# The stick-breaking scores' high-part product: 128 rows with a zero-padded key in place of 64 rows

## The chip, the cores and the metric

The kernel runs on one core of one Trainium2 chip. The metric is the device time of one execution in microseconds, given as the median of several runs. A core has a matrix engine (TensorE, PE in the profile, with its weight loads shown apart as PEld), VectorE (DVE), ScalarE (ACT), GpSimd (POOL) and SyncE (SP), which here issues the weight DMAs. The engines run side by side and wait for each other through semaphores. Matrix products write to PSUM; all other tiles lie in SBUF.

## The reference, cut to what matters

The reference is one layer of a decoder trunk on 512 tokens of width 1024: a mixer of three branches (short convolution, stick-breaking attention, retention) merged under sigmoid gates, a cross-attention into 256 memory tokens, and a squared-ReLU MLP, with norms between. The change touches the scores `z` of the stick-breaking attention, which has 8 heads of 64 features:

```python
for start in range(0, s, SB_BLOCK):              # blocks of 128 queries
    end = start + SB_BLOCK
    z = jnp.einsum('bhtd,bhsd->bhts', q[:, :, start:end], k[:, :, :end]) * scale
    causal = s_idx < t_idx
    log_not = jnp.where(causal, jax.nn.log_sigmoid(-z), 0.0)
    between = lax.cumsum(log_not, axis=3, reverse=True) - log_not
    a = jnp.where(causal, jnp.exp(jax.nn.log_sigmoid(z) + between), 0.0)
    outs.append(jnp.einsum('bhts,bhsd->bhtd', a, v[:, :, :end]))
```

A block of queries sees the keys up to its own end, so the four blocks of a head have scores of 128, 256, 384 and 512 columns.

## The kernel before

**Arithmetic.** Products of float32 values are made from fp32r parts: each operand is kept as a high part (the value rounded to fp32r) and a low part (the rest), and a product is high x high + high x low + low x high. In the projections that is a helper, `mm3` (L232), whose three matmuls have the lines L234, L235 and L236; each has 128 partitions of contraction, 128 columns of weights and up to 512 columns of moving operand. Weight chunks of 512 KB arrive by DMA (L178) and are split into parts by ScalarE (L111) and VectorE (L112) ahead of their use.

**Scores.** A head has only 64 features, so the three terms of its score are made with two matmuls. `sq_done` (L455) writes, for each head of a pair, a tile with the query's high part on the head's own 64 partitions and its low part on the other 64. `sk_done` (L464) writes the key the other way round into `sb_k`: its low part on the head's own 64 partitions, its high part on the others. One matmul of `sb_q` against `sb_k` on all 128 partitions (L487) is therefore the sum of both cross terms. The high x high term comes first (L486), on the head's own 64 partitions alone, from `sb_q` and a third tile, `sb_kh`, with the key's high part. For head 0 of a pair these are partitions 0 to 63, for head 1 64 to 127. In both matmuls the query is the stationary operand (128 columns of weights), and both add into the same tile `z`.

**A step.** `sb_scores` (L479) makes `z` for a head and a block of queries; ScalarE and VectorE turn it into log weights, with a mask of the diagonal on GpSimd twice (`diag`, L474, on `sb_e` and on `sb_suf`) and a running sum between; `sb_transpose` (L505) transposes the weights `sb_suf` on TensorE (`aT`, L510) and splits them; `sb_out` (L525) multiplies them with `sb_v` (L544). There are 8 x 4 steps. They stand in the plan between the projections of the first part (the loop at L785), so that the steps' chains through the other engines run beside projections.

**Order.** The plan is written out by hand, but a scheduler then sets each engine's row by its own estimate of times; it may move instructions of different items past each other. Each engine works its row in order. Tiles come from pools with a fixed number of slots: 29 units of 4 KB for each partition for all that lives long (`unit`, L52), 10 scratch slots of 2 KB (`scr`, L55), and in PSUM four banks each for projections and attention. `sb_kh` is a scratch tile, `sb_q` and `sb_k` are units. A tile whose slot is still in use waits for its last reader.

**Later stages.** Products of 1024 x 256 x 512 under the gates and in the MLP's first half are made in seven smaller products (`seven`, L282, matmuls of 256 columns at L290), 18 double tiles in all (six of gates, twelve of hidden tiles); each takes four scratch tiles, and its consumer one or two more.

Of the kernel before, what the change touches and what calls it, by code (L numbers as in the profile page):

```python
# [15 lines left out]
P = 128  # L16
T = 512          # tokens
D = 1024         # model width
KT = D // P      # feature tiles of the model width
NT = T // P      # token tiles  # L20
MEM = 256
W = 512          # branch width
# [5 lines left out]
CW = 1024        # float32 per partition in one weight chunk (512 KB)  # L28

# columns of the packed small parameters  # L30
C_BG, C_CW, C_CB, C_RG = 0, 24, 36, 40
C_N = 44
UNITS, SCRS = 29, 10         # slots of 4 KB and of 2 KB per partition
RAWS, WBUFS, AHEAD = 3, 11, 2     # weight chunks loaded, parts of them, parts split ahead of their use
G7, U7 = 12, 8      # the first gate tile and the first hidden tile that go through seven products
# [3 lines left out]
def trunk_kernel(ctx: ExitStack, tc: tile.TileContext, x, mem, par, rot, dqd, kdec, g_mix, g_xa, g_mem, g_mlp,  # L39
# [11 lines left out]
    # one size for everything that lives longer than a few instructions: 4 KB per partition  # L51
# [12 lines left out]
    class Split:  # L64
        """[P, n * cols] float32 kept as its two fp32r parts, in units of 4 KB"""
# [49 lines left out]
    class Plain:  # L115
        """a chunk as it is"""
# [9 lines left out]
    class Seven:  # L126
        """two chunks [B11 | B12], [B22 | B21] as the seven right-hand blocks of a product"""
# [32 lines left out]
    class Stream:  # L160
        def __init__(self, entries):
            self.loads = [l for e in entries for l in e.loads]
            self.steps, first = [], 0       # (entry, step, first of its loads, loads needed)
            for e in entries:
                e.first = first
                for i, st in enumerate(e.steps):
                    self.steps.append((e, st, first + (len(e.loads) if i else 1)))
                first += len(e.loads)
                e.last = len(self.steps)
            self.raw = {}  # L170
            self.nd = self.ns = 0

        def load(self, n):
            """trace the loads of the first n chunks"""
            while self.nd < min(n, len(self.loads)):
                raw = wpool.tile([P, CW], F32, name="w_raw", bufs=RAWS)
                t, c = self.loads[self.nd]
                nc.sync.dma_start(out=raw, in_=t[c])  # L178
                self.raw[self.nd] = raw
                self.nd += 1  # L180

        def pump(self, n):
            """trace the loads and splits of the first n steps"""
            while self.ns < min(len(self.steps), n):
                e, fn, need = self.steps[self.ns]
                self.load(max(need, e.first + RAWS))
                e.parts.append(fn([self.raw[e.first + i] for i in range(len(e.loads)) if e.first + i in self.raw]))
                self.ns += 1

    plan = []       # (weight chunks, function that traces the work on them)  # L190
# [4 lines left out]
    def capture(build):  # L195
        """the items that build() adds, taken out of the plan"""
        n = len(plan)
        build()
        got = plan[n:]
        del plan[n:]  # L200
        return got
# [19 lines left out]
    def split(hi, lo, src):  # L221
        """hi + lo = src; src in SBUF or PSUM, float32."""
        act.copy(out=hi, in_=src)
        dve.tensor_tensor(out=lo, in0=src, in1=hi.bitcast(F32), op=ALU.subtract)

    def split_scaled(hi, lo, src, s):
        """hi + lo = src * s, s a power of two"""
        act.activation(out=hi, in_=src, func=AF.Copy, scale=s)
        dve.scalar_tensor_tensor(out=lo, in0=src, scalar=s, in1=hi.bitcast(F32),
                                 op0=ALU.mult, op1=ALU.subtract)  # L230

    def mm3(ps, lh, ll, rh, rl, first, last):  # L232
        """one K tile of a float32 product from its fp32r parts"""
# [7 lines left out]
    def proj_t(ps, w, a, sl=slice(None), nk=8, c0=0):  # L241
        """features on partitions: 128 columns of the chunk against the split activations a"""
# [5 lines left out]
    class Mixes:  # L248
        """the seven left-hand blocks of the split activations a, [P, 4 feature tiles, 256 tokens] each"""
# [6 lines left out]
        def make(self, g):  # L256
            """feature tiles 2 g, 2 g + 1 of the mixed blocks"""
# [24 lines left out]
    def seven(b, a):  # L282
        """two tiles of 128 features x 512 tokens, K = 1024, in seven products of half the size each way
        (Winograd's form); returns the first tile's halves and the second tile"""
# [27 lines left out]
    def proj_m(ps, ws, a, t, k0, nk):  # L312
        """128 tokens on partitions: 512 columns, chunks ws hold K tiles k0, k0 + 1, ..."""
# [8 lines left out]
    def items_m(src, c0, a, done, nt=NT, tok_outer=False):  # L322
        """512 output columns from four chunks; done(t, ps) takes each tile of 128 tokens"""
# [21 lines left out]
    def rstd_of(ms, n):  # L345
        """ms^-0.5 on [P, n]"""
# [4 lines left out]
    def sumsq(src, c, ss, dst):  # L351
        """ss[:, c] = sum of the squares of columns c * 512 ...; dst is scratch"""
# [9 lines left out]
    def norm_begin(key, src):  # L362
        """the left half's sum of squares"""
# [7 lines left out]
    def norm_end(key, src, g_bc):  # L371
        """xn = RMSNorm(src) * g for one tile of 128 tokens"""
# [5 lines left out]
    def norm_T(key, dst, t):  # L378
        """tile t of the normalised tokens, transposed and split"""
# [11 lines left out]
    S = {}          # what the phases hand on  # L391

    # ==== mixer: norm ====
# [25 lines left out]
    def item_t(fn, src, c, a=hT, sl=slice(None)):  # L419
        """one output tile with features on partitions; fn(ps) takes it"""  # L420
# [6 lines left out]
    sec = lambda i: 4 * i       # first chunk of section i of w_in  # L427

    # ==== stick-breaking attention ====
    # v of two heads... [token, tile, head, hi 64 | lo 64]  # L430
    def sv_alloc():
        S["v"] = [unit("sb_v", (P, 2, 4, 2 * SBD)) for _ in range(4)]    # [2 * group + tile pair]
# [17 lines left out]
    # Per head, on 128 partitions: the query's two parts, and the key's two parts the other way round  # L450
    # (their product is the two cross terms); the key's high part once more where the query's is.
    # The low half of a head pair keeps its high parts on partitions 0-63, the other on 64-127.
# [11 lines left out]
    def sk_done(m):  # L464
        def fn(ps):
            k = S["sk", m] = unit("sb_k")
            kh = S["skh", m] = scr("sb_kh", dt=F32R)
            act.copy(out=kh, in_=ps)
            for e, (own, oth) in enumerate(((LO, HI), (HI, LO))):
                act.copy(out=k[oth, e, :], in_=ps[own, :])  # L470
                dve.tensor_tensor(out=k[own, e, :], in0=ps[own, :], in1=kh[own, :].bitcast(F32), op=ALU.subtract)
        return fn

    def diag(ap):  # L474
        """keep s < t in a diagonal block"""
# [3 lines left out]
    def sb_scores(hd, tb):  # L479
        hp, e = divmod(hd, 2)  # L480
        q, k = S["sq", hp], S["sk", hp]
        rows = slice(64 * e, 64 * e + 64)
# [3 lines left out]
        te.matmul(z[:, :s], q[rows, e, tsl], S["skh", hp][rows, :s], start=True, stop=False)  # L486
# [5 lines left out]
        # softplus(z) = max(z, 0) + ln(1 + exp(-|z|))  # L492
# [3 lines left out]
        # suffix sums, the own column included: log of the weight is z - suf  # L496
# [28 lines left out]
    def sb_out(hd, tp):  # L525
        """output columns of token tiles 2 tp, 2 tp + 1 of one head"""
# [5 lines left out]
        ostart = [0, 1] if tp == 0 else [0, 3]       # where the two tiles' blocks start  # L532
# [30 lines left out]
    # ==== short convolution ====  # L563
# [27 lines left out]
    # ==== retention: projections ====  # L591
# [23 lines left out]
    # ==== order of the first part: attention steps between projections ====  # L615
# [28 lines left out]
    # ==== retention: recurrence ====  # L644
# [74 lines left out]
    # ==== branch projections under sigmoid gates ====  # L719
# [28 lines left out]
    def item_t7(fn, src, c, *chunks):  # L748
        """two output tiles in seven products; fn(e, halves, *ws) takes tile e as pairs (columns, source)"""
# [59 lines left out]
    # memory norm  # L809
# [10 lines left out]
    # tiles before G7 in full products, while the mixed blocks are made  # L820
# [9 lines left out]
    # ==== mixer output ====  # L830
# [9 lines left out]
    def proj_norm(src, a, g, after):  # L840
        """x += a @ src (1024 columns), and the norm that follows, tile by tile;
        after: what keeps TensorE at work until the last tile is there"""
# [18 lines left out]
    # ==== cross-attention ====  # L861
# [103 lines left out]
    # ==== squared-ReLU MLP ====  # L965
# [11 lines left out]
    def first_up(last_T):  # L977
        """the first tiles in halves of the tokens"""
# [41 lines left out]
    # ==== last projection and final norm, tile by tile ====  # L1020
# [24 lines left out]
def _tables():  # L1045
    """rotary and decay tables: they depend on the shapes alone"""
# [4 lines left out]
    cos, sin = np.cos(ang).T, np.sin(ang).T                      # [64, T]  # L1051
# [3 lines left out]
    rel = i[None, :] - i[:, None]                                # [j, i] -> i - j  # L1055
# [10 lines left out]
def _pack_t(w):  # L1066
    """[1024, N] -> chunks [N/128, 128, 8 * 128]"""
# [4 lines left out]
def _pack_s(w):  # L1072
    """[1024, N] -> chunks [N/128, 128, 2 * 512]: for 256 columns, halves of K and of the columns:
    [B11 | B12], [B22 | B21]"""
# [6 lines left out]
def _pack_m(w):  # L1081
    """[K, N] -> chunks [(N/512) * (K/256), 128, 2 * 512]"""
# [4 lines left out]
def _pack_b(w):  # L1087
    """[512, N] -> chunks [N/256, 128, 4 * 256]"""
# [60 lines left out]
```

## Time and profile before

| | |
|---|---|
| median of 3 runs | 1045.35 us (1045.32 to 1045.4) |
| span of the profiled execution (first to last instruction, which is all that the page gives of it) | 1043.7 us |
| median less span | 1.65 us |
| TensorE busy | 1027.0 us, 98% of the span |
| weight loads | 887.1 us, 85% |
| VectorE, ScalarE, GpSimd busy | 650.4 us (62%), 498.6 us (48%), 59.4 us (6%) |
| chain that ended last, by engine | PE 97%, DMA 1% |
| chain, lines L486 and L487 | 1% each |

The chain is followed back from the last instruction, at each step to what released it. Matmuls overlap in the pipeline: the durations of neighbours add up to more than the time they take together, so what one of them costs is read from the distance between starts, or from the chain, which counts each piece of time once. In the chain view a run of matmuls of one line is merged into one row with its count.

### The profile page before, as it was taken

What the parts mean: (1) busy time and instruction counts of PE and PEld (TensorE: products, weight loads), DVE (VectorE), ACT (ScalarE), POOL (GpSimd) and SP (SyncE); (2) the same over time, 40 slices, a digit from 0 to 9 for tenths busy, and PEclk for the clock granted to TensorE, in tenths of its full rate; (3) what the DMA queues carried; (4) which work ended last, traced back from release to release, by engine and by line L of the source; (5) the groups of instructions that cost most, each with busy time, mean ns of one, the idle gap of its engine ahead of it and who ended that gap; (6) DMA issues with size and microseconds to landing.
All of it is one profiled execution on the core that took longest, in us unless ns stands there. A gap on an engine that the chain in (4) does not pass through costs nothing.

```text
span 1043.7 us, 14329 instructions
## 1 busy us (share of the span) xinstructions
PE 1027.0 (98%) x5636; PEld 887.1 (85%) x5636; DVE 650.4 (62%) x992; ACT 498.6 (48%) x883; POOL 59.4 (6%) x110
## 2 busy tenths in 40 slices
PE   6999999999999999999999999999999999999997
PEld 4878888888888889998898888899889889989985
DVE  5567767765554597685585456365957566565643
ACT  5455556656633244454464445244425734643741
POOL 1001112221110000000010000000000000000000
PEclk9999999999999999999999999999999999999999
DMA  7321223212222213224645213222212322331322
GB/s 262 102 100 65 78 84 119 81 61 102 70 72 81 81 61 102 96 102 148 220 146 178 81 61 122 81 82 101 102 64 90 110 101 81 118 125 66 107 92 80
DMA packets 29875, 106.33 MB, mean 102 GB/s; under 512 B 3568, under 2 KB 3568, under 8 KB 29808
## 3 DMA queue, kind: packets, MB, share of 16 engines
q1 hardware_dynamic: 27216, 98.05, 26.6%
q10 hardware_dynamic: 2592, 7.37, 2.0%
q8 instruction: 44, 0.72, 0.3%
q14 instruction: 23, 0.19, 0.1%
HBM read 103.31 MB, written 2.10 MB: 101 GB/s over the span
## 4 chain that ended last, share of the span: by engine, by line
PE 97%; DMA 1%; DVE 0%; ACT 0%; SPq 0%; issue 0%; DVEq 0%; POOLq 0%; POOL 0%
PE mm L234 24%; PE mm L235 24%; PE mm L236 24%; PE p L290 17%; PE at L385 1%; PE z L486 1%; PE o L544 1%; PE z L487 1%; PE aT L510 1%; DMA w_raw<-in_w_in_dram 1%; PE xsc L236 0%; PE xsc L234 0%; PE xsc L235 0%; PE ro L691 0%; PE sc L665 0%; PE xpp L927 0%
## 5 line engine op out<-in xcount | busy, mean ns | idle before, releaser
L112 DVE TENSOR_TENSOR w_part<-w_raw,w_part 128x1024 fp32r<-128x1024 f32 (+1 forms) x180 | 210.7, 1175 | 171.3 <-PE mm L235 79.8
L111 ACT CAST w_part<-w_raw 128x1024 fp32r<-128x1024 f32 (+1 forms) x180 | 180.5, 1006 | 139.8 <-PE mm L236 83.9
L234 PE MATMUL mm<-hT_h,w_part 128*128 128x512 f32 (+1 forms) x512 | 193.7, 380 | 0.0
L235 PE MATMUL mm<-hT_l,w_part 128*128 128x512 f32 (+1 forms) x512 | 193.3, 378 | 0.0
L236 PE MATMUL mm<-hT_h,w_part 128*128 128x512 f32 (+1 forms) x512 | 192.9, 377 | 0.0
L290 PE MATMUL p<-mix_h,w_part 128*128 128x256 f32 x576 | 112.2, 283 | 0.5 <-ACT sv_s L297 0.5
L236 PEld LDWEIGHTS mm<-hT_h,w_part 128*128 128x128 f32 x512 | 96.4, 188 | 17.4
L235 PEld LDWEIGHTS mm<-hT_l,w_part 128*128 128x128 f32 x512 | 96.5, 188 | 16.5
L234 PEld LDWEIGHTS mm<-hT_h,w_part 128*128 128x128 f32 x512 | 96.2, 188 | 16.7
L235 PE MATMUL mm<-w_part,u_h 128*128 128x512 f32 x256 | 99.8, 390 | 0.0
L234 PE MATMUL mm<-w_part,u_h 128*128 128x512 f32 x256 | 98.8, 390 | 0.0
L236 PE MATMUL mm<-w_part,u_l 128*128 128x512 f32 x256 | 98.0, 389 | 0.0
L290 PEld LDWEIGHTS p<-mix_h,w_part 128*128 128x128 f32 x576 | 93.4, 192 | 1.4 <-ACT sv_s L297 0.7
L290 PE MATMUL p<-hT_h,w_part 128*128 128x256 f32 x432 | 84.4, 283 | 0.0
L290 PE MATMUL p<-mix_l,w_part 128*128 128x256 f32 x288 | 81.4, 283 | 0.0
L290 PEld LDWEIGHTS p<-hT_h,w_part 128*128 128x128 f32 x432 | 70.1, 192 | 0.8
L111 ACT CAST w_part<-w_mix 128x1024 fp32r<-128x1024 f32 x36 | 37.9, 1052 | 55.5 <-PE mm L235 37.4
L112 DVE TENSOR_TENSOR w_part<-w_mix,w_part 128x1024 fp32r<-128x1024 f32 x36 | 44.0, 1222 | 27.1 <-ACT w_part L111 20.0
L290 PE MATMUL p<-hT_l,w_part 128*128 128x256 f32 x216 | 60.7, 283 | 0.0
L236 PEld LDWEIGHTS mm<-w_part,u_l 128*128 128x128 f32 x256 | 48.1, 188 | 9.8
L235 PEld LDWEIGHTS mm<-w_part,u_h 128*128 128x128 f32 x256 | 48.1, 188 | 9.5
L234 PEld LDWEIGHTS mm<-w_part,u_h 128*128 128x128 f32 x256 | 47.9, 188 | 9.6
(210 smaller groups left out, 1808.5 us busy)
## 6 DMA issues: line engine op xcount, KB each, us to landing
w_raw<-in_w_in_dram SPq DMA_DIRECT2D x52, 512.0 KB, 3.4
w_raw<-in_w_up_dram SPq DMA_DIRECT2D x32, 512.0 KB, 3.5
w_raw<-in_w_down_dram SPq DMA_DIRECT2D x32, 512.0 KB, 3.5
w_raw<-in_w_br_dram SPq DMA_DIRECT2D x12, 512.0 KB, 3.4
w_raw<-in_w_gate_dram SPq DMA_DIRECT2D x12, 512.0 KB, 3.5
w_raw<-in_w_o_dram SPq DMA_DIRECT2D x8, 512.0 KB, 3.8
w_raw<-in_w_xk_dram SPq DMA_DIRECT2D x8, 512.0 KB, 4.5
w_raw<-in_w_xv_dram SPq DMA_DIRECT2D x8, 512.0 KB, 3.5
```

The lines of the kernel that those rows point to most:

```text
L111: act.copy(out=wh, in_=src)
L112: dve.tensor_tensor(out=wl, in0=src, in1=wh.bitcast(F32), op=ALU.subtract)
L234: te.matmul(ps, lh, rh, start=first, stop=False)
L235: te.matmul(ps, lh, rl, start=False, stop=False)
L236: te.matmul(ps, ll, rh, start=False, stop=last)
L290: te.matmul(ps[:, :256], x[:, k, :], y, start=first and k == 0 and i == 0, stop=k == 3 and i == 2, skip_group_check=True)
L385: te.transpose(ps[:, k * P:(k + 1) * P], xn[:, c * P:(c + 1) * P], ident)
L486: te.matmul(z[:, :s], q[rows, e, tsl], S["skh", hp][rows, :s], start=True, stop=False)
L487: te.matmul(z[:, :s], q[:, e, tsl], k[:, e, :s], start=False, stop=True)
L510: te.transpose(aps[:, sb * P:(sb + 1) * P], a[:, sb * P:(sb + 1) * P], ident)
L544: te.matmul(dst, vv, rhs, start=sb == 0 and i == 0, stop=sb == nblk and i == 1, skip_group_check=True)
```

## The change

`sb_kh` becomes a unit with a plane of 512 keys for each head of the pair. A plane holds the key's high part on the head's own 64 partitions and zeros on the other 64, where the query tile has its low part. The high x high matmul then takes all 128 partitions of both tiles. GpSimd writes the zeros, and ScalarE casts the high part in two pieces of 64 partitions instead of one of 128. The unit pool gets a slot more (30), the scratch pool one less (9). Otherwise the diff takes comments out and moves line numbers: L486 and L487 become L488 and L489, L476 becomes L479, and the aT matmuls of L510 are L512.

```diff
-UNITS, SCRS = 29, 10         # slots of 4 KB and of 2 KB per partition
...
+UNITS, SCRS = 30, 9
...
             k = S["sk", m] = unit("sb_k")
-            kh = S["skh", m] = scr("sb_kh", dt=F32R)
-            act.copy(out=kh, in_=ps)
+            kh = S["skh", m] = unit("sb_kh")
             for e, (own, oth) in enumerate(((LO, HI), (HI, LO))):
+                pool.memset(kh[oth, e, :].bitcast(F32), 0.0)
+                act.copy(out=kh[own, e, :], in_=ps[own, :])
                 act.copy(out=k[oth, e, :], in_=ps[own, :])
-                dve.tensor_tensor(out=k[own, e, :], in0=ps[own, :], in1=kh[own, :].bitcast(F32), op=ALU.subtract)
+                dve.tensor_tensor(out=k[own, e, :], in0=ps[own, :], in1=kh[own, e, :].bitcast(F32),
+                                  op=ALU.subtract)
...
-        rows = slice(64 * e, 64 * e + 64)
...
-        te.matmul(z[:, :s], q[rows, e, tsl], S["skh", hp][rows, :s], start=True, stop=False)
+        te.matmul(z[:, :s], q[:, e, tsl], S["skh", hp][:, e, :s], start=True, stop=False)
         te.matmul(z[:, :s], q[:, e, tsl], k[:, e, :s], start=False, stop=True)
```

On TensorE the row of the program is nearly the same. The clearest move is at the fourth step of head 0 (512 score columns; `aT` are the transposes of the third step). Before:

```order
L236 MATMUL mm<-hT_h,w_part 128x512
L510 MATMUL aT<-ident,sb_suf 128x128 x2
L486 MATMUL z<-sb_kh,sb_q 128x512
L487 MATMUL z<-sb_k,sb_q 128x512
L234 MATMUL mm<-hT_h,w_part 128x512
```

and now:

```order
L234 MATMUL mm<-hT_h,w_part 128x512
L512 MATMUL aT<-ident,sb_suf 128x128
L488 MATMUL z<-sb_kh,sb_q 128x512
L512 MATMUL aT<-ident,sb_suf 128x128
L489 MATMUL z<-sb_k,sb_q 128x512
L235 MATMUL mm<-hT_l,w_part 128x512
```

Between the score products of the third step and these stand 28 projection products where there were 24, and the two score products no longer stand next to each other: the second transpose is between them.

On ScalarE, at the key of the second head pair (`mm` is the projection's PSUM tile, `w_part` a weight chunk's high part, `sb_e` the softplus of the step at 256 columns). Before:

```order
L468 CAST sb_kh<-mm 128x512
L470 CAST sb_k<-mm 64x512
L111 CAST w_part<-w_raw 128x1024
L489 ACTIVATE sb_e<-z 128x256
L470 CAST sb_k<-mm 64x512
L490 ACTIVATE sb_e<-sb_e 128x256
```

and now:

```order
L471 CAST sb_kh<-mm 64x512
L472 CAST sb_k<-mm 64x512
L111 CAST w_part<-w_raw 128x1024
L491 ACTIVATE sb_e<-z 128x256
L471 CAST sb_kh<-mm 64x512
L472 CAST sb_k<-mm 64x512
L492 ACTIVATE sb_e<-sb_e 128x256
```

One cast more stands between the softplus' first and second function of the step.

On GpSimd the memsets of the first two head pairs, four of them, stand behind the first norm's work and ahead of all masks. The other two pairs stand among the masks. The third head pair's place before (numbers tell the tiles apart):

```order
L476 AFFINE_SELECT sb_suf_1008<-sb_suf_1008 128x128
L476 AFFINE_SELECT sb_e_1072<-sb_e_1072 128x128
L476 AFFINE_SELECT sb_suf_1078<-sb_suf_1078 128x128
L476 AFFINE_SELECT sb_e_1165<-sb_e_1165 128x128
L476 AFFINE_SELECT sb_suf_1171<-sb_suf_1171 128x128
```

and now:

```order
L479 AFFINE_SELECT sb_suf_1014<-sb_suf_1014 128x128
L479 AFFINE_SELECT sb_e_1078<-sb_e_1078 128x128
L470 MEMSET sb_kh_1157 64x512 x2
L479 AFFINE_SELECT sb_suf_1084<-sb_suf_1084 128x128
L479 AFFINE_SELECT sb_e_1174<-sb_e_1174 128x128
```

Two memsets stand between the two masks of one step.

## Rows read from the trace of the kernel before

**Rows 1.** Page, part 1: busy time, share of the span, instructions.
```profile
PE 1027.0 (98%) x5636; PEld 887.1 (85%) x5636; DVE 650.4 (62%) x992; ACT 498.6 (48%) x883; POOL 59.4 (6%) x110
```

**Rows 2.** TensorE's waits: total us, times, longest us.
```profile
PE at L385 <- DVE xn L376: 9.1, 2, 8.6
PE p L290 <- ACT sv_s L297: 0.5, 1, 0.5
```

**Rows 3.** Stretch with all score products: busy us of each engine (instructions), granted clock, DMA.
```profile
55.00:267.00 212.00, 212.00 (x979) 169.98 (x978) 144.90 (x215) 125.32 (x239) 35.96 (x73) 1.00 0.24 85
```

**Rows 4.** Timeline of TensorE, first score tile: start us, duration us, engine, line, tiles, rows*columns.
```profile
55.20 0.39 PE L234 MATMUL mm<-hT_h,w_part 128*128 128x512 f32 x1
55.52 0.32 PE L486 MATMUL z<-sb_kh,sb_q 64*128 64x128 f32 x1
55.77 0.50 PE L235 MATMUL mm<-hT_l,w_part 128*128 128x512 f32 x1
56.11 0.39 PE L236 MATMUL mm<-hT_h,w_part 128*128 128x512 f32 x1
...
56.80 0.39 PE L236 MATMUL mm<-hT_h,w_part 128*128 128x512 f32 x1
57.03 0.22 PE L487 MATMUL z<-sb_k,sb_q 128*128 128x128 f32 x1
...
57.37 0.39 PE L235 MATMUL mm<-hT_l,w_part 128*128 128x512 f32 x1
```

**Rows 5.** Timeline of the weight loads there; idle time before, in brackets.
```profile
54.98 0.19 PEld L234 LDWEIGHTS mm<-hT_h,w_part 128*128 128x128 f32 x1
55.52 0.18 PEld L486 LDWEIGHTS z<-sb_kh,sb_q 64*128 64x128 f32 x1 [0.35 <-issue]
```

**Rows 6.** Chain of work in four short stretches: start us, us, what.
```profile
62.10 0.31 PE z L486
...
62.95 0.23 PE mm L235
...
68.30 0.36 PE z L486
...
69.27 0.23 PE mm L235
...
74.71 0.42 PE z L486
...
75.80 0.23 PE mm L235
...
81.99 0.26 PE z L486
...
82.79 0.23 PE mm L236
```

**Rows 7.** Chain of 55 to 267 us by line; then 31 products of 256 columns.
```profile
by line: PE mm L235 27.4%; PE mm L236 27.3%; PE mm L234 27.3%; PE z L486 5.1%; PE z L487 4.8%; PE o L544 4.3%; PE aT L510 4.0%
...
423.98 3.72 PE p L290 x31
```

**Rows 8.** Casts and subtraction of the key: count, ns min/median/max, first and last start us.
```profile
L470 ACT CAST sb_k<-mm x8: 577/581/586, 51.3 to 190.6; 64x512 fp32r<-64x512 f32 x8
L471 DVE TENSOR_TENSOR sb_k<-mm,sb_kh x8: 672/688/695, 51.9 to 191.2; 64x512 fp32r<-64x512 f32 x8
...
L468 ACT CAST sb_kh<-mm x4: 585/588/593, 50.6 to 186.3; 128x512 fp32r<-128x512 f32 x4
```

**Rows 9.** GpSimd's largest memset (group: us, mean ns), two masks, and the transpose.
```profile
L87 POOL MEMSET ones<- 128x512 f32 x1 | 0.5, 525 | 0.0
...
111.83 0.29 POOL L476 TENSOR_SCALAR_AFFINE_SELECT sb_e<-sb_e 128x128 f32<-128x128 f32 x1 [0.64 <-DVE sb_e L493]
...
154.04 1.12 POOL L476 TENSOR_SCALAR_AFFINE_SELECT sb_suf<-sb_suf 128x128 f32<-128x128 f32 x1 [1.76 <-ACT sb_suf L501]
...
157.99 0.27 PE L510 MATMUL aT<-ident,sb_suf 128*128 128x128 f32 x1
```

## The prediction

> **What bounds the kernel now.** I read the shares of the page first. TensorE (PE) is busy for 98% of the span [rows 1], so the question is what TensorE does with its time and not whom it waits for. The view of waits confirms this: its list has two entries of any weight, 9.1 us on the first norm at the start and 0.5 us once in the later stage [rows 2]. Next I cut out the stretch in which all 32 attention steps (8 heads, 4 query blocks each) lie, 55 to 267 us. There TensorE is busy for 212.00 of 212.00 us, while VectorE has 145 us of work, ScalarE 125 and GpSimd 36 [rows 3]. Time taken from TensorE's stream in this stretch therefore comes off the end, as long as the other engines keep up with a stream that is some 6% denser.
>
> A busy TensorE can still be a slow one, so I read the distances between the starts of neighbouring products. The first score tile is the lucky place: the scheduler put its two products apart, each alone between projection products of 512 columns, which otherwise start 0.23 us apart. Both write the same 128 columns with the same 128 columns of weights; the first (L486) reads 64 partitions, the second (L487) 128. With L486 in between, the product before it and the product after its follower start at 55.20 and 56.11, 0.91 us; without it that would be 2 x 0.23. It costs 0.45 us. With L487 in between, the same distance is 56.80 to 57.37, 0.57 us: it costs 0.11 us [rows 4]. The weight loads say where the 0.34 us go. In the stream a load begins with the product before its own and is done when its own starts (the load at 54.98 belongs to the product at 55.20). The load of L486 begins only at 55.52, together with its product and after 0.35 us in which the loader stood idle with nothing to wait for [rows 5]; and the 128-row product behind it, started at 55.77, holds the next one off until 56.11, 0.34 us and not 0.23 [rows 4]. So the way into 64 rows and the way out of it each cost time in which nothing overlaps.
>
> **What each pair costs now.** For the other widths the two products stand next to each other or with a transpose between them. I take the distance on the chain from the start of L486 to the start of the second projection product after the pair, less 0.23 us for the first of these [rows 6]: 128 columns 81.99 to 82.79, 0.80 - 0.23 = 0.57; 256 columns 62.10 to 62.95, 0.85 - 0.23 = 0.62; 384 columns 68.30 to 69.27, 0.97 - 0.23 = 0.74; 512 columns 74.71 to 75.80, 1.09 - 0.23 = 0.86. A head has one of each: 2.79 us, and eight heads 22.3 us. As a control, the chain of the whole stretch puts 5.1% and 4.8% of 212 us, 21.0 us, on the two lines [rows 7]; the rest of the way out falls on the product that follows, and on a transpose where one stands between.
>
> **What a pair costs afterwards.** Both products then use 128 rows, as does every other product around them. Their prices in an undisturbed stream: 512 columns 0.23 us (the projections of rows 4); 256 columns 3.72 / 31 = 0.12 us [rows 7]; 128 columns 0.11 us, from L487 above [rows 4]. No 384-column product stands in an undisturbed stream; it lies between 0.12 and 0.23, and I take the middle, 0.175, since columns set the price of its neighbours. A head then costs 2 x (0.11 + 0.12 + 0.175 + 0.23) = 1.27 us. **The gain is 8 x (2.79 - 1.27) = 12.2 us.** The bounds: with 384 columns at 0.23 it is 8 x (2.79 - 1.38) = 11.3 us, with them at 0.12 13.0 us. The multiplication by zero rows adds no columns, and the rows say that columns set the price.
>
> **What is added, and what hides it.** ScalarE casts the key's high part in two pieces of 64 x 512 where it was one of 128 x 512. A cast of 64 x 512 takes 0.58 us and the one of 128 x 512 0.59 [rows 8], so it is 0.57 us more for each of four head pairs, 2.3 us on an engine with 87 us free in the stretch; the first of these casts begins at 50.6 and ends at 51.2 us [rows 8], and the first score product that reads it starts at 55.52, so 4.3 us are in reserve for it and for the weight cast behind it. VectorE's subtraction keeps its size. GpSimd gets eight memsets of 64 x 512. Its memset of 128 x 512 takes 0.53 us [rows 9], which I take for each: 4.2 us on an engine with 176 us free. Four of them stand ahead of all masks, in the shadow of the projections. The other four stand in two pairs among the masks of the diagonal, so a mask and then a transpose can come late. How much that may be: the tight case near there is a mask that ends at 154.04 + 1.12 = 155.16, while the transpose that reads it runs at 157.99, 2.83 us later [rows 9]. A pair of memsets at 1.05 us fits in that, so I take nothing. For the upper bound I let the memsets stretch as the masks do, whose same instruction takes 0.29 us or 1.12 [rows 9]: 2 x (0.53 + 0.83) = 2.7 us, and the reserve shrinks by two shorter steps, 2 x 0.40. Then 2.7 + 0.8 - 2.83 = 0.7 us are missing, twice: 1.4 us. Below nothing it can go by the one late wait of 0.5 us [rows 2], which may vanish in a changed order.
>
> The key's high part moves from the pool of 2 KB slots (10, now 9) to that of 4 KB slots (29, now 30). Up to two or three such tiles live at once, so the small pool has more room in this stage and one slot less in the later ones, and the large pool has one or two less in this stage. TensorE's row shows no projection pulled ahead of or behind a score step for it beyond a few places, so I charge nothing.
>
> **The sum.** The profiled execution spans 1043.7 us; the median of the runs is 1045.35, 1.65 us more, which I keep. 1043.7 - 12.2 = 1031.5 us of span, 1033.2 us as a median.
>
> **The rivals.** *Nothing changes.* If the 0.34 us at 55.5 come from something that stays, the use of the query's tile as weights, say, then the pairs keep their price and the time stays at 1045.4 us. For it speaks that L487, on 128 rows, is as slow as L486 where it directly follows it (at 256 columns 0.62 us for both, 0.31 of it L486's) [rows 6]. Against it speaks that L487 alone costs 0.11 us with the same query tile as weights [rows 4], which leaves only the row count and what precedes it. 3%. The Trainium skill, "TensorE: Matmul & The Clock Gate", section "Why this matters for your kernels", is on the side of this rival: it says that one product on few rows takes the "same time as K=128" and that only several at once gain, so that a change from 64 rows to 128 would be worth nothing either way. By that rule the sum is 0; the trace of this case disagrees, with 0.45 us beside 0.11.
>
> *The memsets bite.* The gain comes, but masks behind memsets, or casts behind the second key cast, make transposes late, and TensorE gets waits that it doesn't have now; two to four times 0.7 us and more give 1034.6 to 1037 us. For it: GpSimd's same mask takes 0.29 or 1.12 us, so something stretches it. Against: 2.83 us of reserve in the tight case. 8%.
>
> *Slower: the scratch pool runs dry in the seven-product stages.* These stages make 18 double tiles (six of gates, twelve of hidden tiles), each taking four scratch slots and one or two more behind it, from a pool that loses one of ten. If each double tile waited for a slot until one cast and one subtraction were through (0.59 + 0.69 us by the rows of the key) [rows 8], 18 x 1.3 = 23 us would come on top: 1045.4 - 12.2 + 23 = 1056 us. It decides from 12.2 / 18 = 0.68 us for each. For it: the one wait of the later part sits just there, 0.5 us on a copy into scratch [rows 2]. Against: that is one wait in 18. 4%.
>
> **Chances.** The forecast, within the bounds of the two prices, 85%; memsets 8%, no effect 3%, slower 4%. The range reaches from 13.0 us of gain and the vanished 0.5 (1045.35 - 13.5 = 1031.9) to 11.3 us less the 1.4 us of late masks (1035.5): **1031.9 to 1035.5 us**. What lies outside is the far end of the memsets' case and the other two, about one in ten. A measurement here can tell 0.2%, 2 us, from no change: faster 0.93, same 0.03, slower 0.04.
>
> **What would show it.** Right: the two score lines in the trace of after stand 0.23 us apart at 512 columns where they stand 0.42 now, their share of the chain falls from 21 us to about 10, the load of the first score product begins with the product before it, and TensorE's list of waits stays empty in the stretch, which ends some 12 us earlier with all later stages moved by the same amount. Wrong in the price: the first score product still starts 0.3 us after its predecessor with 128 rows. Wrong in the cover: new waits of transposes on GpSimd's masks, or of later products on scratch copies.

## The result, and the profile after

The changed kernel takes 1033.85 us (median of 4 runs, 1033.71 to 1033.91), the kernel before 1045.34 us on the same chip: a ratio of 0.989 with a 95% interval of 0.9877 to 0.9902, 11.5 us less. The profiled execution spans 1032.0 us where it spanned 1043.7. The forecast was 1033.2 us.

The page's first part (busy time, share of the span and instructions of each engine) stands beside [rows 1]:

```profile
PE 1015.5 (98%) x5636; PEld 884.9 (86%) x5636; DVE 648.8 (63%) x992; ACT 500.7 (49%) x887; POOL 66.2 (6%) x118
```

TensorE has 11.5 us less of busy time with the same 5636 matmuls, and is busy for the same 98% of the span. Its waits (total us, times, longest), beside [rows 2]:

```profile
PE at L385 <- DVE xn L376: 9.0, 2, 8.5
PE p L290 <- ACT sv_s L297: 0.5, 1, 0.5
```

Nothing has joined the list. Then the stretch with all score products, which now ends near 255.5 us, and all that lies behind it (busy us of each engine with its instructions, granted clock, DMA), beside [rows 3], with the later stages before in the first line:

```profile
267.00:1036.50 769.50, 769.01 (x4462) 680.71 (x4462) 472.47 (x723) 343.14 (x585) 19.50 (x25) 1.00 0.29 101
...
55.00:255.50 200.50, 200.50 (x979) 167.72 (x978) 143.41 (x215) 126.42 (x242) 41.12 (x76) 1.00 0.27 90
255.50:1025.00 769.50, 769.01 (x4463) 680.59 (x4461) 472.38 (x724) 343.53 (x585) 19.06 (x25) 1.00 0.30 101
```

The same 979 matmuls take 200.5 us where they took 212.0. In the 769.5 us behind them TensorE is busy for 769.0, the same as before, and the granted clock is 1.00 in all of these stretches, as in [rows 3]. So the whole gain was made in the attention's stretch, by products that stand closer, and none was given back later.

The first score tile on TensorE (start us, duration us, engine, line, tiles), beside [rows 4]; L488 is the high product, the former L486:

```profile
54.99 0.39 PE L234 MATMUL mm<-hT_h,w_part 128*128 128x512 f32 x1
55.21 0.22 PE L488 MATMUL z<-sb_kh,sb_q 128*128 128x128 f32 x1
55.27 0.45 PE L235 MATMUL mm<-hT_l,w_part 128*128 128x512 f32 x1
55.55 0.39 PE L236 MATMUL mm<-hT_h,w_part 128*128 128x512 f32 x1
```

and its weight load, beside [rows 5]:

```profile
54.99 0.19 PEld L488 LDWEIGHTS z<-sb_kh,sb_q 128*128 128x128 f32 x1
```

From the product before it to the product after its follower it is now 54.99 to 55.55, 0.56 us. Around L487 it was 0.57, around L486 0.91. The load of L488 begins at 54.99, with the product before its own, and is done at 55.18, ahead of the product's start at 55.21. The 0.35 us of idle time are gone.

The chain of work, cut to five short stretches (start us, us to the next piece, what), shows the pairs of the four widths, beside [rows 6]: 256, 384, 512 and 128 columns, and 384 columns once more where the pair stands right behind the products that write `o`, of which the last two have 128 columns and the others 256.

```profile
61.54 0.12 PE z L488
61.66 0.12 PE z L489
61.77 0.23 PE mm L234
...
67.36 0.17 PE z L488
67.53 0.18 PE z L489
67.71 0.23 PE mm L234
...
74.21 0.23 PE z L488
74.45 0.11 PE aT L512
74.56 0.23 PE z L489
74.79 0.23 PE mm L235
...
80.35 0.11 PE z L488
80.46 0.11 PE z L489
80.57 0.29 PE mm L235
80.86 0.23 PE mm L236
...
93.95 0.41 PE o L546 x4
94.36 0.23 PE z L488
94.58 0.17 PE z L489
94.76 0.23 PE mm L234
```

At 256 and 512 columns a product takes 0.12 and 0.23 us, as the projections of those widths do. Two places are dearer than that: behind a 128-column pair the next projection product takes 0.29 us and not 0.23, and the 384-column product behind `o` takes 0.23 where the one at 67.36 takes 0.17. The whole stretch's chain by line, beside [rows 7]:

```profile
by line: PE mm L234 28.8%; PE mm L235 28.8%; PE mm L236 28.8%; PE o L546 4.5%; PE aT L512 4.0%; PE z L488 2.7%; PE z L489 2.5%
```

5.2% of 201 us, 10.4 us, lie on the two score lines, where it was 21.0.

Last the added work on GpSimd and ScalarE (count, ns min/median/max, first and last start us), beside [rows 8, 9]:

```profile
L470 POOL MEMSET sb_kh<- x8: 519/520/522, 26.5 to 176.5; 64x512 f32 x8
L471 ACT CAST sb_kh<-mm x8: 577/582/583, 50.4 to 180.4; 64x512 fp32r<-64x512 f32 x8
```

### The profile page after: what moved, and what is told of

It reads as the page before. It is cut to its first block, busy times and chain, and to the rows that moved or that the text cites. A ratio compares the mean times of both kernels' runs of the same rounds, so it can differ in the third digit from the quotient of the medians.

```text
span 1032.0 us, 14325 instructions
## 1 busy us (share of the span) xinstructions
PE 1015.5 (98%) x5636; PEld 884.9 (86%) x5636; DVE 648.8 (63%) x992; ACT 500.7 (49%) x887; POOL 66.2 (6%) x118
## 4 chain that ended last, share of the span: by engine, by line
PE 97%; DMA 1%; DVE 0%; ACT 0%; SPq 0%; issue 0%; DVEq 0%; POOLq 0%; POOL 0%
PE mm L235 24%; PE mm L234 24%; PE mm L236 24%; PE p L290 17%; PE at L385 1%; PE o L546 1%; PE aT L512 1%; DMA w_raw<-in_w_in_dram 1%; PE z L488 1%; PE z L489 0%; PE xsc L236 0%; PE xsc L235 0%; PE xsc L234 0%; PE ro L693 0%; PE sc L667 0%; PE xpp L929 0%
```

## The experiments

The expectations name the theories by letters. **A:** each change between a product on 64 rows and one on 128 costs about 0.17 us of TensorE's time, into the 64 rows and out of them, whatever the product itself does. A step before the change has two such changes, so there are 64 in the kernel. **C:** the row count is innocent, and the gain comes from what else the diff does: another tile, other pools, another order. A third, **B**, grants that the row count matters, but says that every product on 64 rows is slow by itself, whatever stands beside it.

**The row count alone.** The changed kernel with its padded tile, its memsets and its pools, but the high product on the head's own 64 rows again; the zeros are written and not read.

```diff
-        te.matmul(z[:, :s], q[:, e, tsl], S["skh", hp][:, e, :s], start=True, stop=False)
+        rows = slice(64 * e, 64 * e + 64)
+        te.matmul(z[:, :s], q[rows, e, tsl], S["skh", hp][rows, e, :s], start=True, stop=False)
```

> The changed kernel with one thing undone: the high-part product reads the head's own 64 rows of the padded key again; memsets, two casts, pools and TensorE's row stay as in the changed kernel. Theory A (the price lies in changing between 64-row and 128-row products, once in and once out): 1045.4 us, the whole gain of 11.5 us gone. Rival C (the gain came from the pools or the changed order): about 1033.9 us.

It took 1044.99 us (ratio to before 0.9998, interval 0.9988 to 1.0007). The chain at its step of 256 columns, where L489 is the high product and L490 the cross product:

```profile
61.85 0.31 PE z L489
62.17 0.31 PE z L490
```

These are the 0.62 us of [rows 6] again, 0.39 more than the 0.23 for both in the changed kernel. In this run and in the changed kernel TensorE, VectorE, ScalarE and GpSimd carry out their instructions on the same tiles in the same order from the first to the last, so neither tile nor pool nor order differs. C falls: the row count alone is worth 1044.99 - 1033.85 = 11.14 us, 0.174 us for each of the 64 changes, as a mean of the ways in and out. At most 0.35 us of the gain are left for everything else in the diff.

**Half of it.** The high product on 128 rows in even heads only; odd heads use rows 64 to 127.

```diff
-        te.matmul(z[:, :s], q[:, e, tsl], S["skh", hp][:, e, :s], start=True, stop=False)
+        rows = slice(64 * e, 128)
+        te.matmul(z[:, :s], q[rows, e, tsl], S["skh", hp][rows, e, :s], start=True, stop=False)
```

> The changed kernel with the high-part product on 128 rows for the even heads alone (own rows 0 to 63) and on 64 rows for the odd heads (rows 64 to 127). Theory A: half of the gain stays, 1033.85 + 11.5 / 2 = 1039.6 us. If the price hung on which half of the array is used: 1045.3 us (only the upper half dear) or 1033.9 us (only the lower half dear).

It took 1039.43 us (0.9944, 0.9929 to 0.9959). That is 5.6 us above the changed kernel, half of the 11.14: the cost goes with the number of changes, and the 32 that are left, all in the upper half of the rows, cost what the average of both halves costs.

**The price of one product, on 128 rows and on 64.** To measure the disputed cost by itself, two kernels add to each of the 32 steps of the changed kernel a product of 128 columns whose moving tile is all zeros, between the two score products. The sum stays what it was. The first adds it on 128 rows:

```diff
+    zt = const.tile([P, P], F32R, name="zt")
+    pool.memset(zt.bitcast(F32), 0.0)
...
         te.matmul(z[:, :s], q[:, e, tsl], S["skh", hp][:, e, :s], start=True, stop=False)
+        te.matmul(z[:, :P], q[0:128, e, tsl], zt[0:128, :], start=False, stop=False, skip_group_check=True)
         te.matmul(z[:, :s], q[:, e, tsl], k[:, e, :s], start=False, stop=True)
```

> The changed kernel with a third product into each score tile, between the two: the query as weights, 128 columns of zeros as moving operand, on 128 rows. It adds zero; its price is all it brings. By the single 128-row product of 128 columns in the trace of before, 0.11 us each: 32 x 0.11 = 3.5 us, 1037.4 us, by every theory.

It took 1037.56 us (0.9926, 0.9909 to 0.9942): 3.71 us more than the changed kernel, 0.116 us for each of 32. The second adds it on the head's 64 rows:

```diff
+        te.matmul(z[:, :P], q[64 * e:64 * e + 64, e, tsl], zt[64 * e:64 * e + 64, :], start=False, stop=False, skip_group_check=True)
```

> As the run with the zero product on 128 rows, but the zero product on the head's own 64 rows. Theories A and B: 0.45 us each as the single 64-row product of 128 columns in the trace of before, 32 x 0.45 = 14.4 us, 1048.2 us. If 64 rows cost no more than 128: 1037.4 us as its neighbour.

It took 1048.11 us (1.0027, 1.0016 to 1.0038): 14.26 us more than the changed kernel, 0.446 us for each. The chain at the step of 256 columns, with the added product (L491) between the high product (L490) and the cross product (L492), on 128 rows:

```profile
61.86 0.12 PE z L490
61.98 0.06 PE z L491
62.03 0.17 PE z L492
```

and on 64 rows:

```profile
62.14 0.11 PE z L490
62.25 0.25 PE z L491
62.51 0.31 PE z L492
```

The piece of the added product grows from 0.06 to 0.25 us, that of the next from 0.17 to 0.31: 0.33 us for the way in and the way out together, 0.165 each in the mean. The line's group of weight loads in the kernel on 64 rows (ns min/median/max, and under it the idle time before them, by what ended it, with the number of times) shows that the length of the load is not the reason:

```profile
L491 PEld LDWEIGHTS z<-zt,sb_q x32: 182/183/184, 55.6 to 268.8; 64*128 64x128 f32 x32
...
  issue: 4.6, 20
```

It takes 0.18 us where one on 128 rows takes 0.19, but in front of 20 of the 32 the loader stands idle with nothing to wait for, 0.23 us each in the mean.

**Is it the product or the change?** The same added product on 64 rows, twice in a row. By A the second adds only what a product of 128 columns costs anyhow, by B it costs the full price again.

```diff
+        te.matmul(z[:, :P], q[64 * e:64 * e + 64, e, tsl], zt[64 * e:64 * e + 64, :], start=False, stop=False, skip_group_check=True)
+        te.matmul(z[:, :P], q[64 * e:64 * e + 64, e, tsl], zt[64 * e:64 * e + 64, :], start=False, stop=False, skip_group_check=True)
```

> As the run with one zero product on 64 rows, but with two of them in a row on the same 64 rows. Theory A (the change of row count is what costs): the second one comes at its columns' price, 32 x 0.11 = 3.5 us more than the run with one, about 1051.7 us. Rival B (every 64-row product carries the surcharge, because its weights aren't loaded ahead): 32 x 0.45 = 14.4 us more, about 1062.6 us.

It took 1051.75 us (1.0062, 1.0045 to 1.0078). The second product costs 3.64 / 32 = 0.114 us, the same as one on 128 rows. The chain at that step (L491 and L492 are the added products, L493 the cross product):

```profile
62.02 0.11 PE z L490
62.13 0.25 PE z L491
62.39 0.11 PE z L492
62.50 0.31 PE z L493
```

The second, at 62.39, takes 0.11 us; the first and the product after both take 0.25 and 0.31 as with a single one. The weight loads there (start us, duration us, idle time before in brackets) show the same:

```profile
62.06 0.18 PEld L491 LDWEIGHTS z<-zt,sb_q 64*128 64x128 f32 x1 [0.24 <-issue]
62.17 0.19 PEld L492 LDWEIGHTS z<-zt,sb_q 64*128 64x128 f32 x1
62.43 0.19 PEld L493 LDWEIGHTS z<-sb_k,sb_q 128*128 128x128 f32 x1
```

The load of the second 64-row product follows 0.11 us behind the first, beside the product ahead and without idle time. The load of the 128-row product behind them starts another 0.26 us later. B falls: it is the change that costs, not the 64 rows.

**Fewer changes without padding.** If A holds, the kernel before must gain when its 64-row products stand next to each other. Here the steps of a head are written two at a time: both high products, then both cross products. In the order that results, two high products follow each other at 8 places, six times those of 384 and 512 columns and twice those of 128 and 256 (not 384 and 512 at all eight, as the expectation has it), and stand alone at 16. That makes 48 changes where there were 64.

```diff
+    def sb_products(hd, tbs):
...
+        for tb in tbs:
...
+            te.matmul(z[:, :s], q[rows, e, tb * P:s], S["skh", hp][rows, :s], start=True, stop=False)
+        for tb in tbs:
...
+            te.matmul(S["z", hd, tb][:, :s], q[:, e, tb * P:s], k[:, e, :s], start=False, stop=True)
```

> The kernel before, without any padding, with the products of two steps of a head written together: both on 64 rows first, then both on 128. In TensorE's row the scheduler keeps 8 of the 16 such pairs together (those of 384 and 512 columns), so 48 changes of row count are left of 64, with all 64-row products kept. Theory A: 16 changes at the 0.17 to 0.2 us that the earlier runs gave for one, some 3 us less than before, 1042.3 us, unless score tiles held longer in PSUM bring waits. Rival B (each 64-row product dear by itself): 1045.3 us.

It took 1042.62 us (0.9975, 0.9965 to 0.9985), 2.61 us less than before, 0.163 us for each of the 16 changes that are gone. On the chain (L487 high, L490 cross) four products of 384 and 512 columns stand together, and a step of 128 columns alone:

```profile
67.91 0.60 PE z L487 x2
68.51 0.61 PE z L490 x2
69.11 0.23 PE mm L234
...
81.94 0.26 PE z L487
82.19 0.26 PE z L490
82.45 0.28 PE mm L235
```

The four take 0.60 + 0.61 = 1.21 us. By [rows 6] the two pairs cost 0.74 + 0.86 = 1.60 us apart, and 0.35 + 0.46 = 0.81 on 128 rows. The lone step has the 0.26 and 0.26 us of before. So grouping recovers half of the excess where it takes hold. It needs no zeros, but it cannot reach what padding reaches, since two changes stay in each group.

**The pools alone.** The other part of the diff, in each kernel by itself: the new slots in the kernel before, and the old slots in the changed kernel.

```diff
-UNITS, SCRS = 29, 10         # slots of 4 KB and of 2 KB per partition
+UNITS, SCRS = 30, 9
```

> The kernel before with the changed pool sizes alone (30 units, 9 scratch slots), the key's high part still a scratch tile and the product on 64 rows. Theory A: the pools carry none of the gain, 1045.4 us give or take 0.5. The scratch rival (the later stages wait for the missing slot): several us more than 1045.4; from 0.68 us for each of 18 double tiles it would eat the gain, 1057 us.

```diff
-UNITS, SCRS = 30, 9
+UNITS, SCRS = 29, 10
```

> The changed kernel with the pool sizes of before (29 units, 10 scratch slots), the key's high part still padded in a unit. If the pools carry nothing: 1033.9 us give or take 0.5. If the extra unit was needed for the padded tiles: waits of TensorE in the attention stretch and several us more.

The kernel before took 1045.78 us with the new slots (1.0004, 0.9995 to 1.0014), the changed kernel 1034.37 with the old ones (0.9896, 0.9881 to 0.9911). Both are 0.5 us above their partner (1045.28 and 1033.85), which is less than such a comparison can tell from nothing; from first to last instruction the medians differ by 0.15 and 0.25 us (1043.75 against 1043.6, 1032.35 against 1032.1). The slots carry none of the gain, and the changed kernel doesn't need the extra unit. No variant was faster than the changed kernel.

## Why the prediction was right, and where 0.7 us went

**What bounds the kernel.** Right. TensorE was the bound before and is after, and what its stream lost came off the end one for one: 11.5 us less busy time, 11.5 us less in all.

**The way in and the way out.** Right, and the step that carried everything. It was read from one place in [rows 4], where the scheduler happened to put the two products apart; that such a place exists was luck. Four kernels measure the same change of row count: 0.174 us (64 of them taken back), 0.165 (64 added), 0.163 (16 grouped away), and no further price for a second product in a row. These are means of the way in and the way out, and the 0.34 us that [rows 4, 5] give for the two together are 0.17 each. By this the mechanism is shown as a price of the change; what TensorE does in that time no run shows.

**What each pair costs now, and afterwards.** The 2.79 us a head before the change were read at one step of each width, and stand within a few hundredths. Of the 1.27 us forecast for after, three widths came out to within 0.01 us a product: 256 columns 0.12, 512 columns 0.23, and the middle value for 384 columns, 0.175, beside 0.17 and 0.18. Two were too low, and they are the difference between the 12.2 us forecast and the 11.5 measured:

- *128 columns: 0.22 us forecast for the pair, 0.28 measured.* The two products take 0.11 us each, as forecast, but at the seven steps where the pair stands behind `o` the product behind it takes 0.28 to 0.29 us and not 0.23, some 0.4 us in all. The price before, taken at 81.99 behind `o`, contained this follower; the one afterwards was made from a product that stood alone. There the 0.11 us already hold what the follower pays, and the two products that stand apart in head 0 do cost 0.11 each (55.21 to 55.55 is 0.34 us, 0.11 more than 0.23).
- *384 columns behind `o`: 0.40 us for the pair, not 0.35.* At seven of eight heads the pair stands right behind the last two products of `o`, of 128 columns, and its first product takes 0.23 us, as the row at 94.36 shows; 0.05 us seven times is 0.35 us. Before the change the pair cost hardly more there than in head 0, 0.75 us where the prediction had 0.74:

```profile
96.71 0.37 PE z L486
97.08 0.38 PE z L487
```

Together 0.8 us, so 12.2 - 0.8 = 11.4. At three heads transposes stood ahead of and between the two products of 512 columns before the change too, and the pair cost 0.80 to 0.82 us there and not 0.86, some 0.1 us more to take off; the 0.2 us that the sum is then too low were not taken apart. Both places of the list lie behind products of 128 columns in a row. Such products start 0.11 us apart while the load of 128 x 128 weights takes 0.19 us, and a zero product of 128 columns alone between wide ones takes a piece of 0.06 us (61.98 in the kernel with added products on 128 rows). That the loads fall behind in such a row and the next wide product pays is what fits these rows; it is argued, and no run took it apart.

**What hides the added work.** Right. The memsets take 0.52 us each and the casts of 64 x 512 0.58; GpSimd gained 6.8 us of work and ScalarE 2.1 over the whole span, and TensorE has no new wait. Of the 6.8 us 4.2 are the memsets, which did not stretch (519 to 522 ns); the masks did, from 0.37 to 0.42 us in the mean on `sb_e` and from 0.42 to 0.48 on `sb_suf`, and the spare time covered it. The 1.4 us kept for late masks weren't needed.

**The pools.** Charged at nothing, and worth 0.5 us at most in either direction, by two kernels. Whether these 0.5 us, and the 0.3 us by which the changed kernel on 64 rows is below the kernel before, come from the order or are chance is open; all are below 0.2%.

**The rivals.** *Nothing changes* fell: with the row count alone undone the time is back at 1044.99 us. The Trainium skill, "TensorE: Matmul & The Clock Gate", section "Why this matters for your kernels", whose "same time as K=128" stood on that side, agrees with the runs inside a row of products of the same row count: the second one on 64 rows cost 0.114 us, and one on 128 rows 0.116. A lone one on 64 rows between products on 128 cost 0.446 us, and there the rule doesn't hold. What fits is another page of the Trainium skill, "TensorEngine Tiling (Array Packing)", section "Tiling Modes", by which a change of the tiling mode, and not of the tile alone, drains TensorE; it gives no time, and these runs put 0.16 to 0.17 us beside it. That a drain is what takes this time no run here shows. *The memsets bite* fell with the empty list of waits. *Slower: the scratch pool* fell with the unchanged 769 us of the later stages, where the one wait of 0.5 us still stands and no other is listed, and with the kernel before on nine slots, 1045.78 us.

**What would show it.** The score lines are 0.23 us long at 512 columns, their share is 10.4 us (about 10 forecast), the load of the first score product begins with the product before it, the stretch holds no wait, and it ends 11.5 us earlier.

## What to carry to other kernels

A TensorE that is busy for 98% of the time can still lose time inside it: read the distances between the starts of neighbouring products, against the same operation in a place where it stands undisturbed. In a stream of products on 128 rows, one on 64 rows here cost 0.29 to 0.40 us for its two changes, so fill the unused rows with zeros if a memset off the critical path can write them, or else put such products next to each other. Price a product together with its follower on both sides of the sum, or on neither.

## What the runs showed of the hardware

- A change between products on 64 and on 128 rows cost 0.16 to 0.17 us, as a mean of the ways in and out, both for the added product of 128 columns and over all widths. At single widths the two changes of a step cost 0.29 us (128 columns, 0.57 - 0.28), 0.38 (256), 0.39 (384) and 0.40 (512) together, by [rows 6] and the chain after. What stands ahead plays a part: 0.34 us for the product of 128 columns between wide ones (0.45 - 0.11), 0.29 behind `o`; 0.39 for 384 columns in head 0, 0.35 behind `o` (0.75 - 0.40). The cause of this spread wasn't looked for.
- A second product on 64 rows, right behind the first, cost 0.114 us at 128 columns, as much as one on 128 rows. Which half of the rows it uses made no difference: half of the heads carried half of the cost.
- The weight load on 64 rows took 0.18 us, on 128 rows 0.19. At a change neither this load nor the next one starts early beside the product ahead: there were 0.23 us of idle loader in the mean in front of 20 of 32 loads on 64 rows, and in the stretch shown the load of the 128-row product behind came 0.26 us after the load ahead of it, where the second load on 64 rows came after 0.11.
- Multiplying by zeros cost nothing that shows: 512 columns took 0.23 us with half of the rows zero as with none.
- GpSimd's memset of 64 x 512 took 0.52 us, and of 128 x 512 0.525 [rows 9]: half the rows, the same time.
